# Differential scores: query hi and lo parts stacked on 128 rows, two products in place of three on 64 rows

## The chip, the cores and the metric

The kernel runs on one core of a Trainium2 chip. The metric is the device time of one execution in microseconds. The core has five engines with their own instruction streams: TensorE (PE; its weight loads are listed as PEld), VectorE (DVE), ScalarE (ACT), GpSimd (POOL) and SyncE (SP, which issues the transfers here). TensorE writes its results to PSUM, ScalarE and VectorE move them on to SBUF.

## The reference, cut to what matters

Two layers of an encoder on 256 tokens of width 1024, all in float32. Each layer projects x, runs three attention branches, merges them through gates, and ends with a feed-forward block and layer normalisations. The change is in the differential branch: 8 heads, each with two softmax maps (c) over 64-wide queries and keys.

```
q = _apply_rope(q.reshape(b, s, DIFF_HEADS, 2, DIFF_D), cos, sin)
k = _apply_rope(k.reshape(b, s, DIFF_HEADS, 2, DIFF_D), cos, sin)
...
sc = jnp.einsum('bqhcd,bkhcd->bhcqk', qblk, k).astype(jnp.float32) * scale
p = jax.nn.softmax(sc, axis=-1)
w = (p[:, :, 0] - lambda_full * p[:, :, 1]).astype(v.dtype)
return jnp.einsum('bhqk,bkhe->bqhe', w, v)
```

## The kernel before, in words

Every float32 operand of a product is held as two fp32r parts: hi (the value rounded, made by ScalarE) and lo (the rest, made by VectorE). A product A x B is then three TensorE products accumulated in one PSUM bank: hi x hi, hi x lo, lo x hi (`mm3`, lines 113 to 115). `evac` (lines 117 to 123) makes hi and lo of a PSUM tile, `wload` (lines 104 and 105) of a weight tile that SP has loaded.

Tokens stand in two tiles of 128. For the differential branch the 8 heads of a layer go in four groups of two. `DiffProj.both` projects q, k and v of a group into three PSUM banks (tag "acc", four banks). `DiffProj.finish` copies q and k to SBUF (line 216), rotates them (`rope`, line 352 on), transposes them back into PSUM (line 224), and evacuates q (scaled by 0.125), k and v into three buffers of the ring "att" (12 buffers of 128 x 2 x 512, lines 219 to 227). After the transpose the 64 channels of map 0 stand on partitions 0 to 63 and those of map 1 on 64 to 127, with two heads x 256 tokens along the columns.

`diff_head` (line 431) makes the scores of a head: for each token tile, product and map one matmul of 64 rows (line 441), map 0 on the lower half of the array's rows, map 1 on the upper; the two maps go to two PSUM banks (tag "sm", four banks). Softmax (line 394 on), combination of the maps, transposes (line 406) and the product with v (line 457) follow. `diff_att` runs both heads of a group and transposes the result (line 548).

ORDER (line 52) is the order in which a layer's units are emitted: P finish a group's projection, D its attention, T/K memory, Q/M memory queries and attention, L/U/A the MLA branch (latents; `uq` and `ukv` up-projections, four PSUM banks at once; attention), g/h/e gates and G/H/E branch products. The framework's planner then simulates the program and fixes the order of each engine's queue, respecting the buffer counts that the kernel gives (BUFS, line 44); units overlap, and a head's twelve scores needn't stay together.

Of the kernel before, what the change touches and what calls it, by code (L numbers as in the profile page):

```python
# [17 lines left out]
P = 128  # L18
# [28 lines left out]
EARLY = 1  # L47
# Emission order of a layer's units up to the merged branches. P/D: projections and attention of a pair
# of differential heads; T/K: memory and its keys and values; Q/M: memory queries and attention;
# L/U/A: latents, up-projections and attention of MLA; g G/h H/e E: gate and branch product of  # L50
# memory/differential/MLA for 256 output columns.
ORDER = "P0 T0 L0 K0 Q0 D0 U0 M0 P1 D1 M1 P2 D2 P3 g0 A0 G0 D3 g1 g2 A1 G1 A2 G2 g3 G3 h0 H0 h1 A3 h2 H1 e0 h3 H2 H3 e1 E0 e2 e3 E1 E2 E3"
# [4 lines left out]
def encoder_trunk(ctx: ExitStack, tc: tile.TileContext, x, mem, positions, w_in, b_gate,  # L57
# [26 lines left out]
    def slot():  # L84
        return act.tile([P, 2, 512], F32R, tag="att", bufs=BUFS["att"], name=nm("att"))
# [38 lines left out]

# [1 line left out]
    def carver(t):  # L126
# [26 lines left out]

# [1 line left out]
    def new_xT():  # L155
# [17 lines left out]
    class DiffProj:  # L173
        """q, k and v of two heads of the differential attention."""

# [35 lines left out]
        def finish(self):  # L211
            stage[0] = "diff_proj"
            nats = []
            for t in range(2):
                nat = tmp.tile([P, 512], F32, tag="natd", bufs=BUFS["natd"], name=nm("natd"))
                S.copy(out=nat, in_=self.qk[t])
                rope(nat.rearrange("p (n d) -> p n d", n=8)[:, :, :ROT_D], cos_d, sin_d, t, 8, ROT_D)
                nats.append(nat)
            qT, kT, vh = slot(), slot(), slot()
            for i, d in enumerate((qT, kT)):  # L220
                ps = acc_tile()
                for j in range(2):
                    for t in range(2):
                        PE.transpose(ps[:, j * T + t * P:j * T + (t + 1) * P],
                                     nats[t][:, i * T + j * P:i * T + (j + 1) * P], ident)
                evac(d[:, 0, :], d[:, 1, :], ps, scale=0.125 if i == 0 else None)
            evac(vh[:, 0, :], vh[:, 1, :], self.vv)
            return qT, kT, vh

# [1 line left out]
    def load_memT():  # L231
# [68 lines left out]

    # rotary tables: [cos | cos | sin-pairs] per token tile
    pos_i = init.tile([P, 2], I32, name="pos_i")
# [41 lines left out]
    def rope(v, cos_t, sin_t, t, n, rot):  # L344
        """v: [P, n, rot] view of natural activations, rotated in place."""
        h = rot // 2
        cb = cos_t[:, t:t + 1, :].broadcast_to([P, n, rot])
        s1 = sin_t[:, t:t + 1, :h].broadcast_to([P, n, h])
        s2 = sin_t[:, t:t + 1, h:].broadcast_to([P, n, h])
        r = tmp.tile([P, 256], F32, tag="rope", bufs=2, name=nm("rope"))  # L350
        rv = r[:, :n * rot].rearrange("p (n r) -> p n r", n=n)
        V.tensor_tensor(rv[:, :, :h], v[:, :, h:], s1, ALU.mult)
        V.tensor_tensor(rv[:, :, h:], v[:, :, :h], s2, ALU.mult)
        V.tensor_tensor(v, v, cb, ALU.mult)
        V.tensor_tensor(v, v, rv, ALU.add)

    # per-partition parameter columns
    NR = 60
# [17 lines left out]
    def lambda_setup():  # L376
        """minus lambda of each layer, on every partition."""
        lam_p = icarve(DEPTH, 2, 64)
# [10 lines left out]

# [1 line left out]
    def softmax_exp(ps, st, t):  # L391
        """two maps side by side in ps; exps to SBUF, sums to st[:, t, :]."""
        mx = tmp.tile([P, 2], F32, tag="mx", bufs=4, name=nm("mx"))
        V.tensor_reduce(mx, ps.rearrange("p (m k) -> p m k", m=2), AX.X, ALU.max, negate=True)
        pt = tmp.tile([P, 2, T], F32, tag="pexp", bufs=BUFS["pexp"], name=nm("pexp"))
        for m in range(2):
            S.activation(pt[:, m, :], ps[:, m * T:(m + 1) * T], AF.Exp, bias=mx[:, m:m + 1],
                         accum_out=st[:, t, m:m + 1])
        return pt

    def transpose_probs(mats):
        """mats[t]: [P(q), T(k)] -> hi/lo [P(k), (kt q)]"""
        ps = sm_tile()
# [8 lines left out]
    def attend_pair(q, k, rows):  # L412
        """two heads whose q/k sit side by side; their transposed probabilities, as hi/lo."""
        st = tmp.tile([P, 2, 2], F32, tag="st", bufs=4, name=nm("st"))
# [15 lines left out]

    def diff_head(l, q, k, j, vh, on):
        """head j of a pair; natural normalised output into on[:, t, :]."""
        st = tmp.tile([P, 2, 2], F32, tag="st", bufs=4, name=nm("st"))
        pss = [sm_tile() for _ in range(2)]
        ks = slice(j * T, (j + 1) * T)
        for t in range(2):
            qs = slice(j * T + t * P, j * T + (t + 1) * P)
            for i, (a, b) in enumerate(((0, 0), (0, 1), (1, 0))):
                for m in range(2):
                    rs = slice(m * 64, (m + 1) * 64)  # L440
                    PE.matmul(pss[m][:, t * T:(t + 1) * T], lhsT=q[rs, a, qs], rhs=k[rs, b, ks],  # L441
                              start=i == 0, stop=i == 2)
        pes = [softmax_exp(pss[m], st, m) for m in range(2)]
# [35 lines left out]
    class MlpTokens:  # L479
        """512 hidden columns of the feed-forward, one token tile at a time."""  # L480

# [23 lines left out]

# [1 line left out]
    def ln_params(g, b):  # L507
# [22 lines left out]

# [1 line left out]
    x_in = [x[0, t * P:(t + 1) * P, :] for t in range(2)]  # L532
    for l in range(DEPTH):
        wi = w_in[l]

        def diff_att(g, qkv):
            stage[0] = "diff_att"
            qT, kT, vh = qkv
            ons = []
            for j in range(2):  # L540
                on = tmp.tile([P, 2, P], F32, tag="on", bufs=3, name=nm("on"))
                diff_head(l, qT, kT, j, vh, on)
                ons.append(on)
# [13 lines left out]
        def gate(i, jp):  # L557
            """tanh of half the gate's argument, for 256 output columns (jp) of branch i."""
            stage[0] = "gate"
# [16 lines left out]
        def branch(i, jp):  # L576
            """branch product times its sigmoid gate, added to the merged columns (twice their value)."""
            stage[0] = "branch"
# [220 lines left out]

        # output projection, residual and first normalisation  # L800
        if l + 1 < DEPTH:
# [33 lines left out]

        # feed-forward
        gb = ln_params(ln2_g[l], ln2_b[l])
# [109 lines left out]
```

## Time and profile before

| | |
|---|---|
| median of 3 runs | 1041.27 us (1040.68 to 1043.42) |
| profiled execution: span | 1040.4 us; the page gives no other time for it, and its span is 0.9 us under the median |
| TensorE busy | 1021.8 us, 7333 matmuls |
| VectorE busy | 695.1 us |
| ScalarE busy | 565.4 us |
| DMA moved | 178.18 MB, mean 171 GB/s |

A span runs from the program's first instruction to its last, as the profiler recorded them. "Busy" is the union of an engine's instructions; matmuls overlap in the pipeline, so their durations add to more than the busy time, and the distance between two starts is the time that one of them really takes.

### The profile page before, as it was taken

The numbers are of one execution on the slowest core, as the hardware profiler recorded it, in microseconds if no ns is written. First come the engines' busy times: TensorE is split into PE (matmuls) and PEld (weight loads), VectorE is DVE, ScalarE is ACT, GpSimd is POOL, SyncE is SP. The second block draws the span as 40 slices with busy tenths as digits, with TensorE's granted clock in tenths as the row PEclk, the third lists the DMA queues.
The fourth block names the chain that finished last, engine by engine and source line by source line (L and its number), as shares of the span: only waits on it lengthen the run. The fifth ranks groups of instructions, "written<-read, shape, count | busy, mean of one in ns | idle before, by whom it ended". The sixth has DMA issues, their size and how long they took to land.

```text
span 1040.4 us, 18327 instructions
## 1 busy us (share of the span) xinstructions
PE 1021.8 (98%) x7333; PEld 959.5 (92%) x7333; DVE 695.1 (67%) x1019; ACT 565.4 (54%) x1008; POOL 54.1 (5%) x102
## 2 busy tenths in 40 slices
PE   7999999999999999999999999999999999999996
PEld 7999999999998998899989999999999979999985
DVE  6857778666869665555766687767587876545564
ACT  4757657656554454445624675766566525444440
POOL 0201000000000000000000210100100010000001
PEclk9999999999999999999999999999999999999998
DMA  8966445444557566665745754444455835665631
GB/s 294 306 192 178 126 122 151 134 123 134 171 181 265 154 196 193 185 186 179 247 128 188 235 166 127 137 131 135 122 163 158 271 97 165 210 192 174 192 102 40
DMA packets 132766, 178.18 MB, mean 171 GB/s; under 512 B 6029, under 2 KB 114633, under 8 KB 132681
## 3 DMA queue, kind: packets, MB, share of 16 engines
q1 hardware_dynamic: 132032, 176.71, 56.1%
q8 instruction: 57, 0.93, 0.4%
q10 hardware_dynamic: 648, 0.31, 0.1%
q14 instruction: 29, 0.23, 0.1%
HBM read 174.89 MB, written 2.10 MB: 170 GB/s over the span
## 4 chain that ended last, share of the span: by engine, by line
PE 93%; DMA 3%; DVE 2%; ACT 1%; POOL 1%; issue 0%; POOLq 0%; SPq 0%; DVEq 0%; ACTq 0%
PE mlp2.acc L114 6%; PE mlp1.sm L113 6%; PE mlp1.sm L115 6%; PE mlp1.sm L114 6%; PE mlp2.acc L113 5%; PE mlp2.acc L115 5%; PE gate.acc L115 4%; PE gate.acc L113 4%; PE gate.acc L114 4%; PE diff_proj.acc L113 4%; PE diff_proj.acc L114 4%; PE diff_proj.acc L115 4%; PE branch.acc L113 4%; PE branch.acc L114 4%; PE branch.acc L115 4%; PE diff_att.sm L441 2%
## 5 line engine op out<-in xcount | busy, mean ns | idle before, releaser
L105 DVE TENSOR_TENSOR mlp1.whl<-mlp1.raw,mlp1.whl 128x1024 fp32r<-128x1024 f32 x124 | 151.1, 1225 | 136.5 <-ACT mlp1.whl L104 134.3
L104 ACT CAST mlp1.whl<-mlp1.raw 128x1024 fp32r<-128x1024 f32 x124 | 129.1, 1047 | 152.7 <-PE mlp1.sm L115 69.3
L113 PE MATMUL mlp1.sm<-wout.xT,mlp1.whl 128*128 128x256 f32 x480 | 135.9, 283 | 0.0
L114 PE MATMUL mlp1.sm<-wout.xT,mlp1.whl 128*128 128x256 f32 x480 | 135.8, 283 | 0.0
L115 PE MATMUL mlp1.sm<-wout.xT,mlp1.whl 128*128 128x256 f32 x480 | 135.8, 283 | 0.0
L114 PE MATMUL mlp2.acc<-mlp1.whl,mlp1.att 128*128 128x512 f32 x240 | 94.8, 395 | 0.0
L113 PE MATMUL mlp2.acc<-mlp1.whl,mlp1.att 128*128 128x512 f32 x240 | 94.3, 393 | 0.0
L115 PE MATMUL mlp2.acc<-mlp1.whl,mlp1.att 128*128 128x512 f32 x240 | 94.0, 391 | 0.0
L113 PEld LDWEIGHTS mlp1.sm<-wout.xT,mlp1.whl 128*128 128x128 f32 x480 | 91.7, 191 | 0.6
L114 PEld LDWEIGHTS mlp1.sm<-wout.xT,mlp1.whl 128*128 128x128 f32 x480 | 91.7, 191 | 0.5
L115 PEld LDWEIGHTS mlp1.sm<-wout.xT,mlp1.whl 128*128 128x128 f32 x480 | 91.7, 191 | 0.0
L105 DVE TENSOR_TENSOR gate.whl<-gate.raw,gate.whl 128x1024 fp32r<-128x1024 f32 x48 | 58.6, 1224 | 25.5 <-ACT gate.whl L104 23.9
L105 DVE TENSOR_TENSOR diff_proj.whl<-diff_proj.raw,diff_proj.whl 128x1024 fp32r<-128x1024 f32 x47 | 57.3, 1223 | 22.9 <-ACT diff_proj.whl L104 22.6
L104 ACT CAST diff_proj.whl<-diff_proj.raw 128x1024 fp32r<-128x1024 f32 x47 | 49.2, 1050 | 29.0 <-PE diff_proj.acc L115 15.2
L104 ACT CAST gate.whl<-gate.raw 128x1024 fp32r<-128x1024 f32 x48 | 50.3, 1049 | 20.5 <-PE gate.acc L115 10.1
L113 PE MATMUL diff_proj.acc<-diff_proj.whl,mlp1.xT 128*128 128x256 f32 x192 | 54.8, 287 | 0.5 <-ACT mlp1.xT L119 0.5
L113 PE MATMUL gate.acc<-mlp1.xT,gate.whl 128*128 128x256 f32 x192 | 55.0, 286 | 0.0
L113 PE MATMUL gate.acc<-start.xT,gate.whl 128*128 128x256 f32 x192 | 55.0, 286 | 0.0
L114 PE MATMUL diff_proj.acc<-diff_proj.whl,mlp1.xT 128*128 128x256 f32 x192 | 54.9, 287 | 0.0
L115 PE MATMUL gate.acc<-mlp1.xT,gate.whl 128*128 128x256 f32 x192 | 54.8, 285 | 0.0
L115 PE MATMUL gate.acc<-start.xT,gate.whl 128*128 128x256 f32 x192 | 54.8, 285 | 0.0
L115 PEld LDWEIGHTS mlp2.acc<-mlp1.whl,mlp1.att 128*128 128x128 f32 x240 | 45.1, 188 | 10.3
(355 smaller groups left out, 3010.8 us busy)
## 6 DMA issues: line engine op xcount, KB each, us to landing
mlp1.raw<-in_mlp_w_dram SPq DMA_DIRECT2D x124, 512.0 KB, 4.4
gate.raw<-in_w_in_dram SPq DMA_DIRECT2D x48, 512.0 KB, 3.7
diff_proj.raw<-in_w_in_dram SPq DMA_DIRECT2D x47, 512.0 KB, 4.5
branch.raw<-in_w_branch_dram SPq DMA_DIRECT2D x32, 512.0 KB, 3.6
wout.raw<-in_w_out_dram SPq DMA_DIRECT2D x16, 512.0 KB, 3.8
mem_keys.raw<-in_mem_w_kv_dram SPq DMA_DIRECT2D x8, 512.0 KB, 5.2
mem_vals.raw<-in_mem_w_kv_dram SPq DMA_DIRECT2D x8, 512.0 KB, 6.6
mq.raw<-in_w_in_dram SPq DMA_DIRECT2D x8, 512.0 KB, 5.4
```

Of the source, the lines that this page charges most:

```text
L104: S.copy(out=hl[:, 0, :n], in_=raw[:, :n])
L105: V.tensor_tensor(hl[:, 1, :n], raw[:, :n], f32v(hl[:, 0, :n]), ALU.subtract)
L113: PE.matmul(ps, lhsT=lh, rhs=rh, start=start, stop=False)
L114: PE.matmul(ps, lhsT=lh, rhs=rl, start=False, stop=False)
L115: PE.matmul(ps, lhsT=ll, rhs=rh, start=False, stop=stop)
L441: PE.matmul(pss[m][:, t * T:(t + 1) * T], lhsT=q[rs, a, qs], rhs=k[rs, b, ks], start=i == 0, stop=i == 2)
```

## The change

`finish` now transposes q and k into two PSUM tiles first. It takes four ring buffers: q2, kh, kl and v's. In q2 each map m has 512 columns of its own, in which the map's own 64 partitions (a) hold q's hi part and the other 64 (b) hold q's lo part. kh and kl hold k's hi and lo part of map m twice, on partitions a and again on b. A product of q2 and kh on 128 rows is then hi x hi + lo x hi, and one of q2 and kl is hi x lo + lo x lo. `diff_head` makes these two per map and token tile, map by map. Comments and docstrings fall away as well; BUFS and ORDER stay.

```diff
-            qT, kT, vh = slot(), slot(), slot()
-            for i, d in enumerate((qT, kT)):
+            pst = []
+            for i in range(2):
                 ps = acc_tile()
...
-                evac(d[:, 0, :], d[:, 1, :], ps, scale=0.125 if i == 0 else None)
+                pst.append(ps)
+            rows = (slice(0, 64), slice(64, 128))
+            q2, kh, kl, vh = slot(), slot(), slot(), slot()
+            for m in range(2):
+                a, b = rows[m], rows[1 - m]
+                S.activation(q2[a, m, :], pst[0][a, :], AF.Copy, scale=0.125)
+                V.scalar_tensor_tensor(q2[b, m, :], pst[0][a, :], 0.125, f32v(q2[a, m, :]),
+                                       ALU.mult, ALU.subtract)
+                S.copy(out=kh[a, m, :], in_=pst[1][a, :])
+                S.copy(out=kh[b, m, :], in_=pst[1][a, :])
+                V.tensor_tensor(kl[a, m, :], pst[1][a, :], f32v(kh[a, m, :]), ALU.subtract)
+                V.tensor_tensor(kl[b, m, :], pst[1][a, :], f32v(kh[a, m, :]), ALU.subtract)
             evac(vh[:, 0, :], vh[:, 1, :], self.vv)
-            return qT, kT, vh
+            return (q2, kh, kl), vh
...
-        for t in range(2):
-            qs = slice(j * T + t * P, j * T + (t + 1) * P)
-            for i, (a, b) in enumerate(((0, 0), (0, 1), (1, 0))):
-                for m in range(2):
-                    rs = slice(m * 64, (m + 1) * 64)
-                    PE.matmul(pss[m][:, t * T:(t + 1) * T], lhsT=q[rs, a, qs], rhs=k[rs, b, ks],
-                              start=i == 0, stop=i == 2)
+        for m in range(2):
+            for t in range(2):
+                qs = slice(j * T + t * P, j * T + (t + 1) * P)
+                d = pss[m][:, t * T:(t + 1) * T]
+                PE.matmul(d, lhsT=q2[:, m, qs], rhs=kh[:, m, ks], start=True, stop=False)
+                PE.matmul(d, lhsT=q2[:, m, qs], rhs=kl[:, m, ks], start=False, stop=True)
```

## Rows read from the trace of the kernel before

**Rows 1.** The page: span, busy time, share of the span and instructions of each engine.
```profile
span 1040.4 us, 18327 instructions
...
PE 1021.8 (98%) x7333; PEld 959.5 (92%) x7333; DVE 695.1 (67%) x1019; ACT 565.4 (54%) x1008; POOL 54.1 (5%) x102
```
**Rows 2.** Waits of TensorE, the first three: us in total, times, longest.
```profile
PE start.sm L163 <- DMA start.x<-in_x_dram: 6.9, 2, 4.3
PE mlp1t.sm L499 <- DVE mlp1t.fr L476: 2.3, 1, 2.3
PE latent.sm L665 <- ACT latent.nat L645: 0.5, 1, 0.5
```
**Rows 3.** Window, mq.acc: us; PE, PEld, DVE, ACT busy (count); clock; DMA.
```profile
71.47:82.99 11.52, 11.52 (x96) 11.47 (x95) 0.69 (x1) 0.60 (x1) 1.00 0.63 170
```
**Rows 4.** Groups by shape: count | busy us, mean ns | idle before.
```profile
L441 PE MATMUL diff_att.sm<-diff_proj.att,diff_proj.att 64*128 64x256 f32 x192 | 22.8, 302 | 0.0
```
**Rows 5.** Timeline of TensorE round two whole heads: start us, length us.
```profile
82.87 0.28 PE L115 MATMUL mq.acc<-start.xT,mq.whl 128*128 128x256 f32 x1
83.08 0.98 PE L441 MATMUL diff_att.sm<-diff_proj.att,diff_proj.att 64*128 64x256 f32 x12
83.99 0.45 PE L113 MATMUL uq.acc<-uq.whl,latent.att 128*128 128x384 f32 x1
84.27 0.34 PE L114 MATMUL uq.acc<-uq.whl,latent.att 128*128 128x384 f32 x1
84.45 0.34 PE L115 MATMUL uq.acc<-uq.whl,latent.att 128*128 128x384 f32 x1
...
96.04 0.39 PE L114 MATMUL ukv.acc<-ukv.whl,latent.att 128*128 128x512 f32 x1
96.27 0.40 PE L115 MATMUL ukv.acc<-ukv.whl,latent.att 128*128 128x512 f32 x1
96.51 0.28 PE L457 MATMUL diff_att.sm<-diff_proj.att,diff_att.pT 128*128 128x256 f32 x1
96.72 0.98 PE L441 MATMUL diff_att.sm<-diff_proj.att,diff_proj.att 64*128 64x256 f32 x12
```
**Rows 6.** Timeline of TensorE round six scores of one map.
```profile
128.98 0.28 PE L115 MATMUL mem_att.sm<-mem_att.pT,mem_vals.att 128*128 128x256 f32 x1
129.19 0.97 PE L441 MATMUL diff_att.sm<-diff_proj.att,diff_proj.att 64*128 64x256 f32 x6
130.09 0.39 PE L114 MATMUL diff_proj.acc<-diff_proj.whl,start.xT 128*128 128x256 f32 x1
```
**Rows 7.** Windows round the 30 stretches of scores: first, last, sum.
```profile
82.87:84.27 1.40, 1.40 (x16) 1.13 (x15) 1.40 (x2) 1.08 (x2) 0.00 (x0) 1.00 0.46 162
...
735.98:737.31 1.33, 1.33 (x16) 1.06 (x15) 0.12 (x1) 0.00 (x0) 0.00 (x0) 1.00 1.00 350
sum 33.64, PE 33.64 PEld 25.48 DVE 17.47 ACT 13.55 POOL 1.79; mean PE 1.12 PEld 0.85 DVE 0.58 ACT 0.45 POOL 0.06
```
**Rows 8.** Groups of evacuations by shape.
```profile
L120 DVE TENSOR_TENSOR diff_proj.att<-diff_proj.acc,diff_proj.att 128x512 fp32r<-128x512 f32 x16 | 10.3, 683 | 0.2
L119 ACT CAST diff_proj.att<-diff_proj.acc 128x512 fp32r<-128x512 f32 x16 | 8.6, 604 | 0.0
L754 ACT COPY mla_att.part<-mla_att.sm 64x256 f32<-64x256 f32 x16 | 5.9, 368 | 5.3 <-PE mla_att.sm L742 5.2
L120 DVE TENSOR_TENSOR mla_att.mqk<-mla_att.sm,mla_att.mqk 96x512 fp32r<-96x512 f32 x8 | 5.5, 687 | 1.2 <-ACT mla_att.mqk L119 1.1
```
**Rows 9.** Window: the first layer's attention stretch, all engines (POOL behind ACT).
```profile
20.00:260.00 240.00, 239.51 (x1893) 231.81 (x1892) 170.65 (x288) 155.50 (x334) 20.11 (x40) 1.00 0.57 168
```
**Rows 10.** Timeline at the second finish: VectorE, TensorE.
```profile
122.54 1.28 DVE L120 TENSOR_TENSOR diff_proj.att<-diff_proj.acc,diff_proj.att 128x512 fp32r<-128x512 f32 x2
...
125.22 0.38 PE L441 MATMUL diff_att.sm<-diff_proj.att,diff_proj.att 64*128 64x256 f32 x1
```
**Rows 11.** Timeline: ScalarE evacuates the second memory query tile.
```profile
83.19 0.60 ACT L122 ACTIVATE mq.att<-mq.acc 128x512 fp32r<-128x512 f32 x1 [0.39 <-PE mq.acc L115]
```

More of the change, by code (lines that the diff above doesn't have):

```diff
@@ L429, in attend_pair, with diff_head @@
         return [transpose_probs([pes[t][:, j, :] for t in range(2)]) for j in range(2)]
-    def diff_head(l, q, k, j, vh, on):
+    def diff_head(l, qk, j, vh, on):
         st = tmp.tile([P, 2, 2], F32, tag="st", bufs=4, name=nm("st"))
+        q2, kh, kl = qk
         pss = [sm_tile() for _ in range(2)]
         ks = slice(j * T, (j + 1) * T)
-        for t in range(2):
-            qs = slice(j * T + t * P, j * T + (t + 1) * P)
-            for i, (a, b) in enumerate(((0, 0), (0, 1), (1, 0))):
-                for m in range(2):
-                    rs = slice(m * 64, (m + 1) * 64)
-                    PE.matmul(pss[m][:, t * T:(t + 1) * T], lhsT=q[rs, a, qs], rhs=k[rs, b, ks],
-                              start=i == 0, stop=i == 2)
+        for m in range(2):
[4 more added lines that the diff above has]
+                PE.matmul(d, lhsT=q2[:, m, qs], rhs=kl[:, m, ks], start=False, stop=True)
         pes = [softmax_exp(pss[m], st, m) for m in range(2)]
@@ L537, in diff_att @@
             stage[0] = "diff_att"
-            qT, kT, vh = qkv
+            qk, vh = qkv
             ons = []
@@ L541, in diff_att @@
                 on = tmp.tile([P, 2, P], F32, tag="on", bufs=3, name=nm("on"))
-                diff_head(l, qT, kT, j, vh, on)
+                diff_head(l, qk, j, vh, on)
                 ons.append(on)
```

## The prediction

> **What bounds the kernel now.** Begin with the page: TensorE is busy 1021.8 of 1040.4 us, VectorE 695.1 [rows 1], and the granted clock is 1.00, the upper level of 2.4 GHz, in the windows that I use [rows 3, 7, 9]. A busy share alone would prove little, since matmul ends are modelled, so the next view is the one that lists what TensorE waited for: 6.9 us for the first rows of x, 2.3 us in the last layer's feed-forward, and behind these three lines of at most 0.5 us [rows 2]. No line names the differential attention. TensorE is thus fed without a break, and the kernel lasts as long as its instruction stream takes to issue. What counts for one matmul is therefore not its duration (some 280 ns, overlapped) but the distance from its start to the next one's. Over a stretch that is nothing but 128-row, 256-column products, 96 of them take 11.52 us: 0.120 us each [rows 3].
>
> **What the old scores cost.** There are 192 score products, 64 rows by 256 columns, at line 441 [rows 4]: 16 heads (8 in each layer), two maps, two token tiles, three products. Read their starts. The first score starts 0.21 us after the product before it (82.87 to 83.08), where 0.12 is the pace. The twelve then take 0.91 us to the next foreign start, 0.076 each: they go two at a time, one map on each half of the rows. The foreign product behind them, 384 columns wide, needs 0.28 us to its successor, where the next one needs 0.18 [rows 5]. Six turns of two at 0.12 would be 0.72, so this stretch carries 0.09 + 0.19 + 0.10 = 0.38 us over. Where the order has cut a head apart, so that six products of one map stand alone, nothing is paired: six take 0.90 us, again 0.18 over six turns, with 0.09 ahead (128.98 to 129.19) [rows 6]. So a stretch costs its turns and about 0.38 us for changing from 128-row to 64-row work and back. Other changes of product cost nothing of the kind: from the 512-column product at 96.27 to a 256-column one on another tile takes 0.24 us, its neighbour (96.04 to 96.27) takes 0.23, and only the step into the scores shows 0.21 instead of 0.12 [rows 5].
>
> The scores stand in 30 stretches, 15 in a layer. I put a window round each, from the start of the last foreign product ahead to the start of the second one behind; the 30 windows sum to 33.64 us [rows 7]. Each holds two foreign products at their own pace: 56 of the 60 have 256 columns, two 384, two 128, together 60 x 0.12, or 7.2 us, and some 0.1 for the wider ones. The scores hold TensorE for 33.64 - 7.3 = 26.3 us.
>
> **What the new scores cost.** Per head and layer 2 maps x 2 token tiles x 2 products = 8 instead of 12, on 128 rows: 16 x 8 = 128. At the pace of rows 3 that is 128 x 0.120 = 15.4 us, and no change of row height is left at all. TensorE gains 26.3 - 15.4 = 10.9 us; I carry 11. Note where it comes from: 30 stretches x 0.38 is 11.4 us. In turns there is nothing to gain, because pairs already did two products in one turn. For the new products' pace the row is of the same form (rows, columns, type, one weight load each); its bounds are 0.11, one rounding of the timeline under the pace of rows 3, and 0.152, the turn of an intact stretch (0.91 / 6, rows 5), which make the gain 12.2 and 6.8 us.
>
> The Trainium skill has a rule that speaks against this change. "TensorE: Matmul & The Clock Gate", Part 3 (Packing small matmuls), says that products on different row groups run at the same time in the array, so that two 64-row products cost about one. The trace bears the pairing out inside a stretch (0.076 us each, rows 5). By that rule alone a head would cost 6 turns, 16 x 6 x 0.12 = 11.5 us in all, and the change would lose 3.9 us; the windows measure 26.3 instead, since they contain the entries, the exits and the unpaired stretches.
>
> **What the change adds.** finish() made two instructions each for q and k (line 226), one on ScalarE and one on VectorE; now ScalarE has 6 and VectorE 6. The new ones work on 64 rows, but a duration follows the columns, not the rows: 96 rows of 512 take VectorE 687 ns, 128 rows 683. For ScalarE I take the 604 ns of 128 rows of 512; its 64-row copy of half the columns takes 368. That copy (line 754) also writes the other half of the rows than it reads, so no crossing surcharge shows on ScalarE [rows 8]. VectorE's crossing form is not in the trace; I bound it between the same 0.68 us and twice that, and take 0.68, the nearest row. Per finish ScalarE gets 4 x 0.60 = 2.4 us and VectorE 4 x 0.68 = 2.7 us; over 8 finishes 19 and 22 us. VectorE is busy 170.7 of 240 us in the first layer's attention stretch; four finishes add 10.9 us, from 71 to 76% [rows 9]. What hides it is TensorE's other work. Behind the new instructions on those queues stand the weight splits (lines 104 and 105) and the softmax, and eight buffers of split weights lie ahead of TensorE.
>
> The tightest finish is the second one: VectorE ends its three splits at 122.54 + 1.28 = 123.8 and the first score follows at 125.22, 1.4 us later [rows 10]. With 2.7 us more the scores must come later; the planner that writes the order knows the added instructions and has the next pair's projection to put there. The PSUM bank of q is freed by the fourth VectorE instruction instead of the first, about 2.1 us later, while the next projection needs its second bank 24 products, 2.9 us, after its first. I price this at 0, with 2.7 us a finish as the upper bound.
>
> The ring "att" is the second cost: it keeps its 12 buffers, and a finish takes 4 instead of 3. When the memory queries are evacuated, before: 3 + 3 latents + 2 keys + 2 values + 2 queries = 12, just full. After: 13. The second query tile (its evacuation starts at 83.19 on ScalarE) must wait for the first latent buffer, which uq's products read, and keeps one of the four accumulator banks that uq needs. That costs between nothing (uq fills three banks and takes the fourth when one is copied out) and a quarter of uq's 36 products, 9 x 0.18 (rows 5) = 1.6 us, with as much for ukv, whose second value tile needs the last latent buffer [rows 11]. I take 1 us in each layer, 2 us in all.
>
> **The sum.** On the profiled execution: 1040.4 - 11.0 + 2.0 = 1031.4 us of span. The median of the runs is 1041.27, 0.9 above that span, so I forecast 1041.3 - 9.0 = 1032.3 us.
>
> **Rivals.** (1) The order gets worse: the ring and the later banks cost 4 to 8 us instead of 2, which leaves 1034.3 to 1038.3. For it: the ring was exactly full. Against: rows 2 show that the present order covers tight places everywhere. (2) Slower: the evacuation of q and k becomes TensorE's wait. If a finish's whole 2.7 us of VectorE time showed at each of 8 finishes, 21.6 us, the time is 1041.3 - 11 + 21.6 = 1052; it turns slower than before from 11 / 8 = 1.4 us a finish. For it: the 1.4 us of slack in rows 10. Against: TensorE had no wait at any finish, and 24% of VectorE's time there remains free. (3) The surcharge isn't tied to the row height but to going to these tiles, so that it stays: 128 x 0.12 + 30 x 0.38 = 26.8 us in place of 26.3, and with the 2 us of waits 1043.8. Against: the step at 96.27. (4) The lost pairing decides, as 6 turns against 8 without any surcharge before: 16 x 2 x 0.12 = 3.9 us, 1041.3 + 3.9 + 2 = 1047. Against: the windows. The skill's rule above is this rival.
>
> **How the numbers follow.** About 0.3%, 3.1 us, is what a measurement of this kernel tells from no change. Forecast, 1028 to 1035: 66%. Rival 1 beyond 1035: 14%, nearly all still faster by over 0.3%. Rival 3: 5%, to which I add 5% for waits that eat just about the gain: within 0.3%. Rival 2: 6%; rival 4: 4%. Faster 0.79, same 0.11, slower 0.10. The range runs from 1027.5 (no new wait and the 2.3 us at line 499 gone too [rows 2]: 1041.3 - 11.0 - 2.3 = 1028.0, and 0.5 less) to 1039, which holds rival 1 and a little of the equal case.
>
> **What would show it.** Right: no 64-row product is left; 128 products at the score lines, 0.12 us from start to start, with 0.12 ahead and behind; TensorE's busy time near 1011 us; ScalarE near 585, VectorE near 717. Ring: the second query tile's evacuation far behind its last product, which ends near 83 us before. Rival 2: TensorE idle before scores or projections, released by VectorE at the new lines. The prediction is wrong if the new products stand 0.15 us or more apart, if gaps of 0.2 us remain round them, or if TensorE's waits grow by more than 8 us.

## The result, and the profile after

The changed kernel is slower. It takes 1049.03 us (median of 4 runs, 1048.07 to 1049.33) against 1042.0 for the kernel before on the same chip: ratio 1.0059, 95% interval 1.0042 to 1.0075. The profiled spans are 1046.3 and 1040.4 us, 5.9 apart. The forecast was 1032.3, its range 1027.5 to 1039.

The page after, span and engines:

```profile
span 1046.3 us, 18241 instructions
...
PE 1016.5 (97%) x7269; PEld 958.2 (92%) x7269; DVE 715.4 (68%) x1051; ACT 579.4 (55%) x1040; POOL 56.1 (5%) x102
```

TensorE is busy 5.3 us less than before, VectorE 20.3 and ScalarE 14.0 us more [rows 1]. The timeline of TensorE round the first head, which answers to [rows 5]:

```profile
84.38 0.28 PE L115 MATMUL mq.acc<-start.xT,mq.whl 128*128 128x256 f32 x1
84.50 0.28 PE L455 MATMUL diff_att.sm<-diff_proj.att,diff_proj.att 128*128 128x256 f32 x1
84.62 0.28 PE L456 MATMUL diff_att.sm<-diff_proj.att,diff_proj.att 128*128 128x256 f32 x1
...
85.33 0.28 PE L456 MATMUL diff_att.sm<-diff_proj.att,diff_proj.att 128*128 128x256 f32 x1
85.44 0.34 PE L113 MATMUL uq.acc<-uq.whl,latent.att 128*128 128x384 f32 x1
```

Eight scores from 84.50 to 85.44, 0.94 us or 0.118 each, 0.12 ahead and nothing extra behind: the scores do what was forecast. The loss is in the view that was nearly empty before [rows 2], the waits of TensorE:

```profile
PE start.sm L163 <- DMA start.x<-in_x_dram: 7.1, 3, 4.1
PE diff_proj.acc L113 <- DVE ukv.att L120: 4.9, 2, 3.5
PE branch.acc L113 <- ACT mla_att.o L771: 2.2, 1, 2.2
PE load_memT.acc L113 <- DVE gate.gt L612: 1.8, 2, 1.6
PE mlp1t.sm L513 <- DVE mlp1t.fr L490: 1.6, 1, 1.6
PE latent.sm L679 <- ACT latent.nat L659: 1.3, 2, 1.1
PE branch.acc L114 <- DVE mla_att.o L772: 0.6, 1, 0.6
```

Four kinds are new or grown. One is in the middle of a layer (the next group's projection behind `ukv`'s evacuations), two at a layer's end (branch products, and output products, which the view lists as `load_memT.acc`, behind the MLA head and the gates), one soon after the first finish (`latent.sm`). I added up all start-to-start distances of TensorE and took each product's usual distance off. What lies over it in gaps above 0.2 us is 8.6 us before and 22.8 after (14.1 more before rounding); stretches at the lower clock cost 1.0 more; everything else, the score products among it, is 9.2 less. That is the 5.9.

TensorE's waits of over 0.15 us sum to 10.4 us before and 21.3 after, so one of the prediction's own signs of being wrong, more than 8 us of new waits, has come.

None of these waits is at a differential head. The one wait that names a line of the change is 0.4 us at 36.4 us, behind VectorE at line 235. The evacuations that the change adds [rows 8] cost what was forecast, 687 to 689 ns on VectorE and 579 to 592 on ScalarE (groups by shape: count | busy us, mean ns | idle before):

```profile
L235 DVE SCALAR_TENSOR_TENSOR diff_proj.att<-diff_proj.acc,diff_proj.att 64x512 fp32r<-64x512 f32 x16 | 11.0, 689 | 0.6
L240 DVE TENSOR_TENSOR diff_proj.att<-diff_proj.acc,diff_proj.att 64x512 fp32r<-64x512 f32 x16 | 11.0, 688 | 0.2
L239 DVE TENSOR_TENSOR diff_proj.att<-diff_proj.acc,diff_proj.att 64x512 fp32r<-64x512 f32 x16 | 11.0, 687 | 0.6
L234 ACT ACTIVATE diff_proj.att<-diff_proj.acc 64x512 fp32r<-64x512 f32 x16 | 9.5, 592 | 0.3
```

What they do is fill the engines in the stretch where two finishes and their heads fall together. First the kernel before, then the changed one, in the same window (columns as in [rows 9]):

```profile
140.00:180.00 40.00, 40.00 (x340) 39.06 (x337) 29.26 (x52) 26.46 (x62) 3.29 (x8) 1.00 0.45 129
```

```profile
140.00:180.00 40.00, 40.00 (x340) 40.00 (x339) 35.69 (x63) 30.70 (x70) 4.14 (x8) 1.00 0.51 145
```

VectorE goes from 73 to 89% of that stretch; the forecast had 76% as the mean over 240 us, where it is 75. From a finish's first transpose to its last evacuation it is now 8.2, 9.3 and 10.2 us in the second to fourth finish of the first layer, where it was 5.0, 5.4 and 6.9. TensorE is still busy all of that stretch. The planner's order brings other products forward: by 260 us it has begun 432 of the layer's 576 gate products, against 394 before. That is the bill's other half. In the kernel before, the window from the first product behind the first layer's last MLA head up to 302.10 us shows

```profile
296.43:302.10 5.67, 5.67 (x50) 5.67 (x49) 2.40 (x4) 2.88 (x7) 0.00 (x0) 1.00 0.66 194
```

50 products: the last two of the head itself, still running, and 48 gate products, which need nothing of that head and cover the time until its result is evacuated. After the change the last head's products come at 302.0 instead of 296.3 us, the last gate product of that stretch at 300.6 instead of 303.3, and no gate product is left behind the head (57 before, in each layer). In the first layer branch products on earlier heads' results cover most of the time, and 2.7 us of waits remain. In the second layer it is plain (timeline of TensorE after; the bracket is the idle time and its releaser):

```profile
818.20 0.99 PE L756 MATMUL mla_att.sm<-mla_att.pT,ukv.att 128*128 128x256 f32 x7
821.36 0.74 PE L113 MATMUL branch.acc<-mla_att.o,branch.whl 128*128 128x256 f32 x4 [2.16 <-ACT mla_att.o L771]
```

The ring shows too. The second memory query tile is evacuated at 92.0 us in the first layer and at 601.28 in the second; its last product starts at 84.38 in the first layer, 7.6 us earlier. Before it was 83.19 [rows 11] and 591.59. (Tile view, ScalarE, with first and last start; and timeline.)

```profile
L122 ACT ACTIVATE mq.att<-mq.acc x2: 590/594/597, 78.9 to 92.0; 128x512 fp32r<-128x512 f32 x2
```

```profile
601.28 0.59 ACT L122 ACTIVATE mq.att<-mq.acc 128x512 fp32r<-128x512 f32 x1
```

The up-projections' evacuations come late behind it, and the next group's projection waits for them, 3.54 us in the second layer; the granted clock falls to 0.50 in that wait (timeline; windows as above):

```profile
612.72 0.58 PE L113 MATMUL diff_proj.acc<-diff_proj.whl,mlp1.xT 128*128 128x256 f32 x1 [3.54 <-DVE ukv.att L120]
```

```profile
600.00:611.00 11.00, 9.18 (x51) 7.85 (x49) 10.25 (x20) 10.07 (x26) 0.36 (x2) 1.00 0.57 155
611.60:618.40 6.80, 5.68 (x27) 5.68 (x27) 2.73 (x9) 1.54 (x7) 0.91 (x2) 0.50 0.50 145
```

### The profile page after: what moved, and what is told of

It reads as the page before. It is cut to its first block, busy times and chain, and to the rows that moved or that the text cites. A ratio compares the mean times of both kernels' runs of the same rounds, so it can differ in the third digit from the quotient of the medians.

```text
span 1046.3 us, 18241 instructions
## 1 busy us (share of the span) xinstructions
PE 1016.5 (97%) x7269; PEld 958.2 (92%) x7269; DVE 715.4 (68%) x1051; ACT 579.4 (55%) x1040; POOL 56.1 (5%) x102
## 4 chain that ended last, share of the span: by engine, by line
PE 90%; DVE 3%; ACT 3%; DMA 2%; issue 1%; POOL 1%; SPq 0%; POOLq 0%; DVEq 0%; ACTq 0%
PE mlp2.acc L114 6%; PE mlp1.sm L113 6%; PE mlp1.sm L115 5%; PE mlp1.sm L114 5%; PE mlp2.acc L113 5%; PE mlp2.acc L115 5%; PE diff_proj.acc L113 5%; PE diff_proj.acc L115 4%; PE diff_proj.acc L114 4%; PE gate.acc L114 4%; PE gate.acc L115 4%; PE gate.acc L113 4%; PE branch.acc L113 3%; PE branch.acc L115 3%; PE branch.acc L114 3%
## 5 line engine op out<-in xcount | busy, mean ns | idle before, releaser
L105 DVE TENSOR_TENSOR mlp1.whl<-mlp1.raw,mlp1.whl 128x1024 fp32r<-128x1024 f32 x124 | 149.0, 1223 | 89.9 <-ACT mlp1.whl L104 88.4
L104 ACT CAST mlp1.whl<-mlp1.raw 128x1024 fp32r<-128x1024 f32 x124 | 126.7, 1046 | 95.5 <-PE mlp1.sm L115 45.0
L104 ACT CAST gate.whl<-gate.raw 128x1024 fp32r<-128x1024 f32 x48 | 50.3, 1053 | 27.1 <-PE branch.acc L115 10.4
L113 PE MATMUL diff_proj.acc<-diff_proj.whl,mlp1.xT 128*128 128x256 f32 x192 | 56.1, 293 | 4.0 <-DVE ukv.att L120 3.5
L114 PE MATMUL diff_proj.acc<-diff_proj.whl,mlp1.xT 128*128 128x256 f32 x192 | 55.8, 291 | 0.0
L115 PE MATMUL diff_proj.acc<-diff_proj.whl,mlp1.xT 128*128 128x256 f32 x192 | 55.5, 291 | 0.0
```

Of the source, the lines that this page charges most:

```text
L104: S.copy(out=hl[:, 0, :n], in_=raw[:, :n])
L105: V.tensor_tensor(hl[:, 1, :n], raw[:, :n], f32v(hl[:, 0, :n]), ALU.subtract)
L113: PE.matmul(ps, lhsT=lh, rhs=rh, start=start, stop=False)
L114: PE.matmul(ps, lhsT=lh, rhs=rl, start=False, stop=False)
L115: PE.matmul(ps, lhsT=ll, rhs=rh, start=False, stop=stop)
```

## The experiments

All runs are against the kernel before on the same chip. Theory A: the ring of 12 buffers is too small for a finish of four. Theory B: the added evacuations cost TensorE time. Theory D says how B can cost it although TensorE is busy beside them: projection, evacuation, scores, softmax and the next group are one serial chain, which becomes longer than the filler (products that need nothing of it) that the order has for the layer's end. Theory C, in the expectations of e1 to e4: the planner's order is fragile, and any edit shifts it. The rivals: the scores themselves, VectorE's load, some other buffer. With the maximum left out of all attentions (e6 to e8) the MLA heads' exponentials are not finite; these three have no time, and e10 and e13 take it out of the differential heads alone.

| run | median us | ratio to before, 95% interval |
|---|---|---|
| change | 1049.03 | 1.0059 [1.0042, 1.0075] |
| e1 change, ring 16 | 1043.77 | 1.0016 [1.0003, 1.0029] |
| e2 before, raw 5 | 1041.93 | 0.9990 [0.9981, 0.9999] |
| e3 before, four buffers a finish | 1062.22 | 1.0187 [1.0173, 1.0200] |
| e4 before, 6 + 6 evacuations | 1050.88 | 1.0079 [1.0065, 1.0092] |
| e5 lean | 1030.99 | 0.9885 [0.9867, 0.9902] |
| e9 change, shared tile of k's lo | 1039.43 | 0.9973 [0.9962, 0.9984] |
| e10 change, ring 13, heads without maximum | 1031.59 | 0.9896 [0.9883, 0.9909] |
| e11 lean, ScalarE evacuates 6 times | 1047.36 | 1.0040 [1.0026, 1.0053] |
| e12 lean, VectorE evacuates 6 times | 1057.53 | 1.0141 [1.0125, 1.0156] |
| e13 before, heads without maximum | 1041.86 | 0.9992 [0.9983, 1.0001] |
| e14 lean, gt 3 | 1031.38 | 0.9888 [0.9874, 0.9901] |
| e15 change, other head of ORDER | 1034.42 | 0.9915 [0.9902, 0.9929] |
| e16 e9 with another ORDER | 1032.05 | 0.9889 [0.9871, 0.9906] |
| e17 before, order of e15 | 1045.29 | 1.0027 [1.0017, 1.0037] |

**The ring by itself (e1).**

```diff
-BUFS = dict(raw=6, whl=8, whlx=4, att=12, o=6, ...)
+BUFS = dict(raw=6, whl=8, whlx=4, att=16, o=6, ...)
```

> The changed kernel with one edit: 16 buffers in the ring att instead of 12. Theory A (the ring): the changed kernel's score products gave TensorE back the 11 us as forecast, and the fourth buffer per finish takes more than that through one chain: the second memory query tile is evacuated some 8 us late (601.3 instead of 591.6 us), its accumulator bank and the value tiles' come free late, the second projection waits (1.5 us at 104, 3.7 us at 612.7), TensorE's clock falls to its lower level for 6.8 us, and all later attention units follow late, so that the branch products at the layers' ends wait for the last MLA head (3.6 and 2.8 us). With 16 buffers all of this goes: 1031 to 1036 us, ratio to the kernel before 0.990 to 0.995; query evacuation right behind its products. Theory B (the evacuations): four more ScalarE and four more VectorE instructions a finish hold accumulator banks and delay the heads; 16 buffers change nothing: 1046 to 1050 us, ratio 1.004 to 1.008. Theory C (the order is fragile, any edit shifts it): anything between, with waits at new places.

1043.77 us: 5.3 less than the change. TensorE's waits from the second line on (this run's profiled execution was its fastest, 1042.05):

```profile
PE mlp1t.sm L513 <- DVE mlp1t.fr L490: 2.4, 1, 2.4
PE branch.acc L113 <- ACT mla_att.o L771: 2.2, 1, 2.2
PE latent.sm L679 <- ACT latent.nat L659: 1.8, 1, 1.8
PE load_memT.acc L113 <- DVE gate.gt L612: 1.6, 1, 1.6
PE branch.acc L114 <- DVE mla_att.o L772: 0.6, 1, 0.6
```

The line with `ukv.att` is gone, and those at the layers' ends and after the first finish stay. The time fits neither A's forecast (1031 to 1036) nor B's (1046 to 1050). It lies between, as C allowed, but without the waits at new places that C expected. Theory A is true, and not enough.

**Each suspect alone in the kernel before (e2 to e4).** To have room, raw (staging buffers for weights) went from 6 to 5 in all three; e2 has nothing else.

```diff
-            qT, kT, vh = slot(), slot(), slot()
-            for i, d in enumerate((qT, kT)):
+            qT, kh, kl, vh = slot(), slot(), slot(), slot()
+            for i, d in enumerate(((qT[:, 0, :], qT[:, 1, :]), (kh[:, 0, :], kl[:, 0, :]))):
...
-                evac(d[:, 0, :], d[:, 1, :], ps, scale=0.125 if i == 0 else None)
+                evac(d[0], d[1], ps, scale=0.125 if i == 0 else None)
```

(e3; the scores take k's parts from kh and kl.)

```diff
-                evac(d[:, 0, :], d[:, 1, :], ps, scale=0.125 if i == 0 else None)
+                for a in (slice(0, 64), slice(64, 128)):
+                    for _ in range(i + 1):
+                        evac(d[a, 0, :], d[a, 1, :], ps[a, :], scale=0.125 if i == 0 else None)
```

(e4.)

> Control: the kernel before with 5 instead of 6 staging buffers for weights. It is what the next two runs are compared with, since their kernels find room in SBUF only so. All theories: the kernel before within 3 us, 1039 to 1045. More than 4 us off would speak for theory C.

> The control with one edit: k's hi and lo parts stand in two buffers of the ring att instead of one, so a finish takes 4 of the 12 as in the changed kernel; every instruction stays (12 score products of 64 rows, two evacuations each for q and k). Theory A: slower than the control by 10 to 17 us, with the late second query evacuation, the wait of the second projection and the waits at the layers' ends. Theory B: the control within 2 us. Theory C: some change of either sign, without the late query evacuation.

> The control with one edit: q and k are evacuated in 6 instructions on ScalarE and 6 on VectorE, on 64 rows each, as often and as long as in the changed kernel (q's halves once each, k's halves twice each over the same place); ring, layout and score products stay. Theory A: the control within 3 us. Theory B: slower than the control by 10 to 17 us, with TensorE waiting on accumulator banks behind the finishes. Theory C: some change of either sign.

raw 5 costs nothing. Four buffers a finish cost 20 us in the kernel before, more than the 10 to 17 expected and nearly four times what the change loses by them, and with the same wait; the second memory query tile is evacuated at 89.4 us, where the scores that follow its products start at 81.9. TensorE's waits of e3, second and third line:

```profile
PE diff_proj.acc L113 <- DVE ukv.att L120: 6.6, 2, 3.3
PE branch.acc L113 <- ACT mla_att.o L757: 2.4, 1, 2.4
```

The waits are 12 us of the 20. The clock adds to them: in e3's profile it is 0.50 in four stretches within the layers, 17.0 us together, where the kernel before has 3.4.

The evacuations alone cost 9 us in the kernel before, a little under the 10 to 17 expected, in waits of the layers' ends and the one after the first finish (branch behind `mla_att.o` 2.4, `latent.sm` behind `latent.nat` 1.5, layer norm behind `branch.xn` 1.3 us). Theory B is true, too. In e4 k's halves are made twice over the same place, so that ScalarE also waits for VectorE there (7.5 us in all, 0.4 in the change); its 9 us are therefore a neighbour of the change's price and not that price itself.

**The change without both (e5).** The old finish, the old ring, and eight products of 128 rows a head out of the tiles that the old finish makes. What they compute is not the reference's scores; the kernel is there for its time, as are e11, e12 and e14.

```diff
-            for i, (a, b) in enumerate(((0, 0), (0, 1), (1, 0))):
-                for m in range(2):
...
+                for i in range(2):
+                    PE.matmul(d, lhsT=q[:, m, qs], rhs=k[:, i, ks], start=i == 0, stop=i == 1)
```

> The kernel before with the new score products alone: finish, its evacuations and its three ring buffers stay as before, and the scores are 8 products of 128 rows a head, q's part m by k's hi and lo parts (its scores are therefore not the reference's; sizes and counts are those of the changed kernel). It shows what TensorE's 11 us are worth with neither the ring nor the evacuations charged. Theory A+B (ring and evacuations are separate costs beside a full gain): 1030 to 1032 us, ratio 0.989 to 0.991. Theory D (the attention units of a layer form one serial chain, scores, maximum, exp, transposes, product, unit after unit, which lies only some 6 us a layer under TensorE's work; what TensorE saves beyond that, or what lengthens the chain, shows at the layer's end): the gain of 5.5 us a layer still fits in the 6 us, 1031 to 1035 us, but the last MLA product with v stays within 3 us of before's 296.3 us, while the last gate product ends some 5 us earlier than before's 303.3.

1030.99 us, 11.6 less than before; TensorE is busy 1010.7 us. All of its gain is there when nobody has to prepare the operands, and the waits are those of [rows 2]:

```profile
PE start.sm L163 <- DMA start.x<-in_x_dram: 7.3, 2, 4.2
PE mlp1t.sm L498 <- DVE mlp1t.fr L475: 2.3, 1, 2.3
PE diff_proj.acc L113 <- ACT mlp1.xT L119: 0.5, 2, 0.2
```

In one point theory D was wrong here: it expected the last MLA product to stay within 3 us of 296.3. It comes at 290.0 us, 6.4 earlier, and so does the last gate product (296.9), with 57 gate products behind the head as before. A saving on TensorE alone therefore brings the chain forward with the filler. What is left of D is that a longer chain runs out from under the filler.

The bill is -11.6 us (scores), +12.8 (e1 less e5: the new finish with its evacuations) and +5.3 (change less e1: the ring). It adds up by construction, since each term is the difference of two runs; by the ratios to the kernel before, the last two are 13.7 and 4.5. That they are two costs is what e3 and e4 show.

**Fewer evacuations (e9).** k's lo parts of both maps in one tile of 512 columns: 6 on ScalarE and 4 on VectorE, and three and a half buffers.

```diff
-            q2, kh, kl, vh = slot(), slot(), slot(), slot()
+            q2, kh, vh = slot(), slot(), slot()
+            kl = act.tile([P, 512], F32R, tag="kl", bufs=2, name=nm("kl"))
...
-                V.tensor_tensor(kl[a, m, :], pst[1][a, :], f32v(kh[a, m, :]), ALU.subtract)
-                V.tensor_tensor(kl[b, m, :], pst[1][a, :], f32v(kh[a, m, :]), ALU.subtract)
+                V.tensor_tensor(kl[a, :], pst[1][a, :], f32v(kh[a, m, :]), ALU.subtract)
```

(The scores then read `kl[:, ks]`; raw is 5.)

> A leaner form of the change. The second product of map 0 needs only q's hi rows against k's lo rows; what k's lo of map 1 adds on the other 64 rows is a product of two lo parts, as small as the lo x lo that the change adds anyway. So one tile of 512 columns holds k's lo of both maps: VectorE makes it on 64 rows once for each map (4 instructions a finish for q and k where the change has 6; ScalarE keeps 6), and a finish takes 3 ring buffers again plus this half one. The 128 products of 128 rows are the same, and the ring's 12 buffers hold the memory queries as before. raw is 5 for space, which cost nothing in the control. By the theory that the ring and the evacuations together ate the gain: no ring wait (ukv.att releases nothing), 8 instructions on VectorE less in a layer than with the change. If VectorE's share of the evacuations is what costs, half of it is left: (1031.0 + 1043.8) / 2 = 1037. If ScalarE's is, or the length of the chain, about 1043. A rival, that the ring was harmless and the stacking itself slow, would leave 1049.

1039.43: a real gain over the kernel before, 4.3 us less than with a large ring, and still 8.4 above the lean kernel. The first finish no longer delays `latent.sm`, but the layers' ends still wait: 2.6 us behind `mla_att.o`, 1.4 behind `branch.xn`, 1.1 behind `gate.gt`. It lies nearer to "VectorE's share" (1037) than to "ScalarE's or the chain" (1043) and decides nothing between them.

**Which engine (e11, e12, with e14 as control).** The lean kernel with only one engine's evacuations made six of 64 rows; gt (buffers for gates) had to go from 4 to 3.

```diff
+                halves = (slice(0, 64), slice(64, 128))
...
-                evac(d[:, 0, :], d[:, 1, :], ps, scale=0.125 if i == 0 else None)
+                for a in halves:
+                    for _ in range(i + 1):
+                        S.activation(d[a, 0, :], ps[a, :], AF.Copy, scale=sc)
+                V.scalar_tensor_tensor(d[:, 1, :], ps, sc, f32v(d[:, 0, :]), ALU.mult, ALU.subtract)
```

(e11; e12 has the loop round VectorE's instruction in place of ScalarE's. e14 is the lean kernel with gt 3.)

> The lean kernel of 1031.0 us (old finish with two instructions for q and k on each engine, 128 products of 128 rows, ring of 12; scores not the reference's) with only ScalarE's evacuations made six of 64 rows instead of two of 128, as the change has them; VectorE keeps two. gt is 3 for space. 8 x 4 x 0.58 = 18.6 us more on ScalarE. If the cost lies on ScalarE, all of the 12.8 us between the lean and the ring-16 kernel: 1043. If on VectorE: 1031 to 1033. If it is the latency from the transpose to the scores, whichever engine: about half, 1037.

> The lean kernel with only VectorE's evacuations made six of 64 rows instead of two of 128; ScalarE keeps two. 8 x 4 x 0.69 = 22 us more on VectorE. If the cost lies on VectorE: 1043. If on ScalarE: 1031 to 1033. If in the latency whichever engine: about half, 1037.

> Control: the lean kernel of 1031.0 us with three buffers gt instead of four, as in the two runs with extra evacuations on one engine (1047.4 and 1057.5). If those lost by the evacuations: 1031 to 1033. If by the gates' buffer: 1045 or more.

What was expected of the two engines fell, on either theory. ScalarE's alone cost 16.0 us over the control, VectorE's alone 26.2, each more than both together in e1 (12.8). gt 3 by itself costs nothing. In e12 the heads came out from under the cover in the middle of the layers as well, and the clock fell behind these waits (windows of e12):

```profile
249.00:257.20 8.20, 5.59 (x34) 4.24 (x34) 5.81 (x9) 5.41 (x17) 0.88 (x2) 0.89 0.50 132
```

```profile
255.40:262.20 6.80, 5.71 (x25) 5.12 (x25) 2.15 (x7) 2.77 (x10) 0.00 (x0) 0.50 0.00 0
```

So either engine is enough, and the price is no sum of instructions: it depends on what the planner's order leaves uncovered. Why one engine's alone cost more than both was not settled. The length of a finish doesn't order them: from first transpose to last evacuation it takes 7.4 to 7.5 us in e11 (second to fourth of the first layer), less than e1's 9.3 to 10.2, and e11 is still the slower. A share of theory C stays possible here, and whether three gate buffers make an uncovered chain dearer is open as well.

**The chain shortened (e10, with e13 as control).** The maximum leaves the softmax of the differential heads, two VectorE instructions of 686 ns and one step of the chain a head; it changes nothing for TensorE or the evacuations.

```diff
...
-        V.tensor_reduce(mx, ps.rearrange("p (m k) -> p m k", m=2), AX.X, ALU.max, negate=True)
...
+        if mx_on:
...
+            V.tensor_reduce(mx, ps.rearrange("p (m k) -> p m k", m=2), AX.X, ALU.max, negate=True)
...
-        pes = [softmax_exp(pss[m], st, m) for m in range(2)]
+        pes = [softmax_exp(pss[m], st, m, False) for m in range(2)]
```

(e10 also has att 13 for 12; e13 is the kernel before with this edit alone.)

> The change with a ring of 13 buffers, without the maximum in the softmax of the 16 differential heads (the exponentials take the scores as they are; MLA and memory keep theirs). It takes two VectorE instructions of 0.685 us and a step of the chain out of every head, 16 x 2 x 0.685 = 21.9 us of VectorE, about what the change adds there, and nothing from TensorE. If the evacuations cost because the attention of a layer is one serial chain (projection, evacuation, scores, softmax, transposes, next group) whose end comes out from under TensorE's other work: the waits at the two layers' ends go (branch behind mla_att.o, output behind gate.gt: 5.7 us in the ring-16 run), the last MLA head's product comes 4 us or more earlier than 300.2 us, and the time is 1035 to 1039. If they cost by holding accumulator banks or by the first finish alone, which has no softmax beside it: 1042 to 1044, as with the ring alone.

> Control: the kernel before without the maximum in the softmax of the 16 differential heads. If the chain of attention steps costs only where it ends out from under TensorE's other work, it is worth at most what TensorE waits at the layers' ends of the kernel before (well under 3 us): 1040 to 1042.5. If the maximum costs TensorE time by itself in any kernel (VectorE's load, or the banks it holds), the same 10 us as in the changed one: 1030 to 1034.

The control stays at 1041.86 (0.9992): in the kernel before, these instructions are free. In the changed kernel they are worth 12 us (1031.59 against e1's 1043.77), more than the 1035 to 1039 expected. The last MLA head's products come at 287.4 us instead of 300.2 in e1, gate products follow until 300.9, and the waits at the layers' ends are gone; that after the first finish, which has no softmax beside it, stays:

```profile
PE start.sm L163 <- DMA start.x<-in_x_dram: 6.7, 3, 4.1
PE mlp1t.sm L514 <- DVE mlp1t.fr L491: 1.6, 1, 1.6
PE latent.sm L680 <- ACT latent.nat L660: 1.3, 2, 1.1
```

This fits theory D, but VectorE's load fell by 20 us as well (696.5 us busy, 716.7 in e1).

**The chain started earlier (e15, with e17 as control).** Every instruction of the change, the ring of 12; only the order's head differs (and gt 3).

```diff
-ORDER = "P0 T0 L0 K0 Q0 D0 U0 M0 P1 D1 M1 P2 D2 ..."
+ORDER = "P0 T0 L0 K0 D0 P1 Q0 M0 M1 D1 U0 P2 D2 ..."
```

> The change with every instruction of it and the ring of 12; only the head of ORDER is other: 'D0 P1 Q0 M0 M1 D1 U0 P2' for 'Q0 D0 U0 M0 P1 D1 M1 P2', so that the first differential heads and the second projection come ahead of the memory queries and the up-projections (gt 3 for space). The memory queries are then evacuated when the first finish's four buffers are about to come free, and the chain of heads starts earlier. By the chain theory: no long wait on ukv.att, waits at the layers' ends under 3 us instead of 6, and 1034 to 1040, although VectorE and ScalarE do as much as with the change. If VectorE's total load is the cost: 1042 or more. If gt of 3 costs, waits on gate.gt of more than 3 us at the layers' ends.

> Control: the kernel before with the head of ORDER and the gt of 3 of the run that gave 1034.4 us with the change. If the order only uncovers the change's own gain, since nothing waits in the kernel before: 1040 to 1044. If the order is worth 8 to 15 us by itself: 1027 to 1035.

1034.42 us, with VectorE busy 715.5 us as in the change, and just as full in the same window. The last MLA head comes at 295.0 us instead of 302.0, and TensorE goes on without a gap behind it (windows of e15):

```profile
295.10:301.00 5.90, 5.90 (x51) 5.90 (x50) 2.55 (x5) 3.86 (x7) 0.00 (x0) 1.00 0.53 149
140.00:180.00 40.00, 40.00 (x340) 40.00 (x339) 35.01 (x61) 31.49 (x67) 2.62 (x8) 1.00 0.48 136
```

```profile
PE latent.sm L679 <- ACT latent.nat L659: 2.1, 2, 1.8
PE mlp1t.sm L513 <- DVE mlp1t.fr L490: 1.5, 1, 1.5
PE latent.acc L113 <- DVE diff_proj.att L235: 0.8, 1, 0.8
```

So neither VectorE's load nor the number of evacuations is the cause by itself: it is where the chain stands against TensorE's filler. Since `Q0` and `U0` now come later, the ring's wait is gone as well, with 12 buffers; this run takes away A and D together. But the ring alone is e1, and e15 is 9.3 us below e1, so most of what it gains is not the ring's. What remains against the lean kernel, 3.4 us, is about the waits of the first finish (0.8 + 2.1). The order itself is no gain: the kernel before gets 2.6 us slower by it (1045.29, just beyond the 1040 to 1044 expected; its waits are no longer, but TensorE is busy 1025.5 us in place of 1021.8, and the distances over the 64-row products, which this order sets otherwise, sum to 24.6 us in place of 20.7). In this order the change is worth 1045.3 - 1034.4 = 10.9 us: nearly 4 us more on TensorE than in the old order, less the waits that stay.

**A better kernel (e16).** e9's shared tile, v evacuated ahead of q and k, the order's head of e15, and gate products moved towards the layer's end (also gt 3, pT 1, which is one buffer of transposed probabilities in place of two, and raw 5).

```diff
+ORDER = "P0 T0 L0 K0 D0 P1 Q0 M0 M1 D1 U0 P2 D2 P3 g0 A0 g2 G0 D3 g1 A1 A2 G2 g3 h0 H0 h2 h1 G3 G1 e0 e3 H1 h3 A3 H2 e1 E0 H3 e2 E1 E2 E3"
```

> A candidate for a kernel better than both: the shared tile of k's lo parts (1039.4 us by itself), v evacuated ahead of q and k, and an order that starts the heads earlier and keeps gate products for after the MLA heads. Chain theory: the last MLA head ends before the last gate products, no wait at the layers' ends, the full gain: 1030 to 1034. If only a part of the waits goes: 1035 to 1038.

1032.05 us, 1.1% under the kernel before, with the maximum kept. With so many edits at once it parts no causes. Its waits are 1.1 us at `latent.sm`, 0.9 at a branch product, and those that the kernel before has. Against the lean kernel (1031.0) 1.1 us are left, less than the half width of the interval (0.2%).

One count parts all the runs that have a trace: the gate products that begin after the last MLA head's last product. They are 57 in each layer before, in e2, e5, e14 and e17, 77 in e13, 96 in e10, 49 in e15, 34 and 23 in e16. There TensorE's waits at branch products, output products and layer norm behind that head sum to 0.9 us at most over both layers. In the change, e1, e3, e4, e9, e11 and e12 the count is 0 in both layers, and these waits sum to 3.7 to 6.5 us. They are a part of the price only: e1's profile has 6.1 us more of all named waits than e5's, and its span is 10.9 us longer.

## Why the prediction was wrong

**The scores: right.** 11.0 us were forecast for TensorE, and e5, which has only this part, gained 11.6. The products stand 0.118 us apart, and no gap remains round them. The rival of the surcharge that stays (3) and that of the lost pairing (4) are thereby out. What decided was the way in and out of the stretches and the unpaired ones. The Trainium skill's rule on products of different row groups ("TensorE: Matmul & The Clock Gate", Part 3) agrees with the trace inside a stretch, 0.076 us a product [rows 5]. The remark that 30 x 0.38 = 11.4 us is where the gain comes from meets the gain by accident: 96 paired turns (11.5) and 11.4 make 22.9 of the 26.3 us, the other 3.4 are, by this estimate, the unpaired stretches', and the new scores take 3.9 more than 96 turns. TensorE's busy time in the change is 1016.5 us, not near 1011 as forecast; in e5 it is 1010.7. The 27 products at the lower clock, 0.21 us each, make up some 2.5 us of the difference by estimate, and the rest was not followed up.

**The ring: right in kind, too small.** The mechanism and the place were as forecast (13 buffers wanted, the second memory query tile late, `ukv` late), the size was not: 2 us forecast, 5.3 measured (change less e1; 4.5 by the ratios). The estimate priced the banks that `uq` lacks. What came on top is that the memory query tile holds up its followers: the evacuations of `ukv` were late, and the next group's projection, which the text didn't follow up to, waited 4.9 us in all, and 6.8 us at half clock came with the longer wait.

**The evacuations: the failed step.** "I price this at 0, with 2.7 us a finish as the upper bound." With the new finish they cost 12.8 us (e1 less e5), 1.6 a finish, inside the bound, over the 1.4 at which rival 2 said the sign turns. The durations and the counts were right (forecast 717 and 585 us of busy time, measured 715 and 579); the step from there was not. The text looked for the cost at the finish and beside its scores, found TensorE covered there, and it was covered. What it left out is that cover is a stock. At the first layer's end the kernel before had 5.67 us of products in hand; the planner's order spent them earlier, beside the longer finishes, and the wait came 100 us or more behind the instructions that caused it, as a wait on MLA heads and gates that the change doesn't touch. Rival 2 named the right side and cause, and the wrong place: of its eight finishes only the first showed a wait.

**The sum's logic.** "TensorE is fed without a break, and the kernel lasts as long as its instruction stream takes to issue" is true of the kernel before and was used for the kernel after. The saving by itself did no harm to that: in e5 the chain's end moved forward with the filler's, 6.4 us each. It is the longer chain that left the cover. e13 and e10 show the edge: the same instructions are worth 0 us on one side of it and 12 on the other.

**The confidence.** 0.10 for slower was too little beside two unknowns of which the text itself said that one was "just full" and the other had 1.4 us of slack.

## What to carry to other kernels

When one engine is busy without a break, ask what the others' chain has in hand where the stage ends: list what the bound engine still has to do behind the last link, and weigh added latency against that stock, not against the work beside it. A ring that is exactly full should be counted with the order of the allocations before and after; here another order of the units took its wait away as more buffers did. And try the saved part alone with the preparation left out: if that run shows the full gain, the loss lies in the preparation and its place in the order.

## What the runs showed of the hardware

A wait can cost TensorE more than its length. In the windows above the granted clock is 1.00 up to 611 us and 0.50, 1.2 GHz, from 611.6 to 618.4: it fell within the wait of 3.54 us that ended at 612.72, and 27 products ran at the lower level. e12 shows the same 6.8 us at 0.50 behind a stretch in which TensorE was busy 5.59 of 8.20 us. In the changed kernel the wait of 2.16 us that ended at 821.36 left the clock at 1.00, while in the kernel before 3.4 us at 0.50 begin at 853.8, within a wait of 2.29 us at line 499. And VectorE takes no surcharge for writing the other half of the partitions than it reads, which the trace before couldn't show: 688 ns across (line 240), 687 straight (line 239).
